# HGRN values in a decoder layer on one Trainium2 core: blocks read back from memory and transposed on VectorE, in place of TensorE transposes

## The chip, the core and the metric

The kernel runs on one core of one Trainium2 chip. The metric is the device time of one execution in microseconds (us). All arithmetic is in 32-bit floats; TensorE products are made of two-part splits of their operands (a rounded part and the rest), three matmuls for each block.

Short names: PE is TensorE (matmul, and the transpose as a matmul with an identity), PEld its weight load, DVE is VectorE, ACT is ScalarE, POOL is GpSimd, SP is SyncE, which issues the DMAs here.

## What is computed

One inference step of a decoder layer, for a prompt of T = 1024 tokens and for 8 single-token samples (NT = 1032 columns together, ND = 8):

```
proj = rmsnorm(x) @ w_in                      # 1024 -> q, f, i, g, z, xbc, dt
f = lb + (1-lb)*sigmoid(f);  k = 1-f;  q = silu(q);  v = i
# HGRN2, 8 heads of 128 x 128: gated linear recurrence
S_t = f_t * S_{t-1} + k_t v_t^T;    o_t = S_t^T q_t
o = rmsnorm(o) * silu(g)
# Mamba-2 SSD, 16 heads, conv + scan -> y
x = x + concat(o, y) @ w_out
x = x + (silu(conv(gate)) * val) @ w_down     # ConvFFN
```

The outputs are y, the new HGRN and SSM states, and the conv states. The change concerns v of the HGRN heads.

## The kernel before

**Layout.** Activations lie feature-major: partitions are features, columns are the 1032 tokens. The input projection is cut into jobs of 128 output features. A job has three chunks of 344 columns, and for each chunk 24 matmuls `mm<-hh,wh`, `mm<-hl,wh`, `mm<-hh,wl` (line 93). `head_in(h)` (L800) makes four jobs for HGRN head h: f, q, v and sg. Each evicts its chunks by an ACT activation (L812); the f job ends with `f_end`, which makes k.

**A head.** `head(h, t)` (L823) is a generator that works through one head in stages. It starts with the 8 decode columns of v: a transpose on PE into the bank vd (L828), a DVE copy (L836), a DMA to memory `vd_d<-vd` (L837), and later two loads `vb<-vd_d` that spread the rows over all partitions for the sample states. Then the 1024 prompt columns of v: eight PE transposes of 128x128 (L833), four to a PSUM bank `vtp`, and two ACT copies of 128x512 (L834) into `vt[0]` and `vt[1]`: token-major blocks, partitions are the 128 tokens of a block and columns its 128 features.

The head then multiplies q by f (L895, DVE, into v's buffer, as v is no more needed), and builds the masked score blocks `am` level by level: products and scalings on DVE (L866, L867, L872), small matmuls `a` on PE, masks on DVE (L891, L902). After them come the transposes of k, and `vt` is used for the first time as the right-hand side of the state matmuls `kv` (L952), later as the left-hand side of the output matmuls `o` (L977). The head ends with its own RMS norm: POOL multiplies twice (L996), and SP writes the result, `mix_d<-sg` (L1001).

**What sets the order.** PE's order is written out by hand: `drive` (L266, called at L1113) advances the head's generator and, at each `yield w`, lets a share of the projection's matmuls go between. Next to head h stand the jobs of head h+1. Next to head 7 stand the first jobs of the output projection, o8.0 to o12.2 (`out_job`). The other engines' orders are set by the scheduler, each engine's instructions run in that order, and so do the DMA issues on SP.

**Output projection.** `o8.0` is the first job that reads `mix_d`, the concatenated mixers' outputs, blocks 8 to 11 of 128 features (the SSM part). `mix_load` fetches four blocks k0 to k3 in three column chunks each: twelve loads `ml<-mix_d` of 172 KB (L175), each split by an ACT cast `mh<-ml` (L1011) and a DVE subtraction `ml<-ml,mh` (L1012). The buffers are those of `hh` and `hl`, which become free as the last projection job (sg of head 7) ends with them. `fetch` is a DMA on SP that is placed after the latest weight load; a weight load is `ws` (L189, 512 KB), with an ACT cast `wh<-ws` (L190) and a DVE subtraction `wl<-ws,wh` (L192).

The functions that the diff touches, and what calls them:

Of the kernel before, what the change touches and what calls it, by code (L numbers as in the profile page):

```python
# [8 lines left out]
F32 = mybir.dt.float32  # L9
# [7 lines left out]
P = 128  # L17
DM = 1024
T = 1024
# [5 lines left out]
H = 8  # L25
SH = 16
CHUNK = 128
NC = T // CHUNK
# [22 lines left out]
def hybrid_layer(  # L51
# [9 lines left out]
    V, A, G, PE, SP = nc.vector, nc.scalar, nc.gpsimd, nc.tensor, nc.sync  # L61
# [5 lines left out]
    dram = ctx.enter_context(tc.tile_pool(name="dscr", bufs=1, space=DRAM))  # L67
# [3 lines left out]
    def nm(s):  # L71
        cnt[0] += 1
        return f"{s}_{cnt[0]}"
# [8 lines left out]
    def tl(tag, name, dt=F32):  # L82
        w, n = TAGS[tag]
        return (work if tag in ("hT", "big", "e", "g") else tmp).tile([P, w], dt, tag=tag, bufs=n, name=nm(name))

    def half(name):
        return tl("s", name)[:, :512]

    def bank(s, tag="mx"):
        return psmx.tile([P, 512], F32, tag=tag, bufs=NBANK[tag], name=nm(s))  # L90
# [65 lines left out]
    ident = keep.tile([P, P], F32, name="ident")  # L156
# [15 lines left out]
    def fetch(dst, src):  # L172

        with tc.issue_after(last_w[0].ins):
            SP.dma_start(dst, src)  # L175
# [50 lines left out]
    def job(name, load, run):  # L226
        jobs.append((name, load, run))
# [51 lines left out]
    def w_in(off):  # L279
        return lambda: wload(w_in_[0, :, off:off + P], KT)  # L280

    def steps(w, m0, m1, hi, lo, cs, out):
        kt = len(hi)
        for k in range(kt):
            for i, (a, x) in enumerate(((w[0], hi), (w[0], lo), (w[1], hi))):
                mm(out, a[:, k, m0:m1], x[k][:, cs], start=(k == 0 and i == 0), stop=(k == kt - 1 and i == 2))
                if k < kt - 1 or i < 2:
                    yield True

    def in_job(name, off, evict, begin=None, end=None):  # L290
        def run(w):
            if begin is not None:
                begin()
            for c, cs in enumerate(chunks):
                ps = psmm.tile([P, 512], F32, tag="mm", name=nm("mm"))[:, :CH]
                yield from steps(w, 0, P, hT_hi, hT_lo, cs, ps)
                evict(c, cs, ps)
                if c == NCH - 1 and end is not None:
                    end()
                yield True  # L300
        job(name, w_in(off), run)

    def in_job_last(name, off, evict, begin):

        def run(w):
            begin()
            ps = [psmm.tile([P, 512], F32, tag="mm", name=nm("mm"))[:, :CH] for _ in chunks]
            for k in range(KT):
                for c, cs in enumerate(chunks):
                    for i, (a, x) in enumerate(((w[0], hT_hi), (w[0], hT_lo), (w[1], hT_hi))):  # L310
                        mm(ps[c], a[:, k, :], x[k][:, cs], start=(k == 0 and i == 0), stop=(k == KT - 1 and i == 2))
                        if k < KT - 1 or i < 2:
                            yield True
                    if k == KT - 1:
                        evict(c, cs, ps[c])
                        yield True
        job(name, w_in(off), run)
# [109 lines left out]
    for c, cs in enumerate(chunks):  # L427
        ps = psmm.tile([P, 512], F32, tag="mm", name=nm("dt"))
# [9 lines left out]
    for i in range(9):  # L438
        n = P if i < 8 else ND
# [85 lines left out]
    for g in range(4):  # L525
        rows = slice(32 * g, 32 * g + 32)
# [203 lines left out]
    def once(work):  # L730
        def run():
# [19 lines left out]
    G.affine_select(eye8, eye8, pattern=[[1, ND], [-1, ND]], compare_op=ALU.is_equal, fill=0.0, base=0,  # L751
                    channel_multiplier=0)
    vd_d = dram.tile([H, ND, P], F32, name="vd_d")

    am = const.tile([P, NC, P], F32, name="am")
    G.memset(am, 0.0)
# [10 lines left out]
    blk = [slice(i * P, (i + 1) * P) for i in range(4)]  # L767
# [32 lines left out]
    def head_in(h):  # L800
        t = {}

        def f_end():
            f, k = t["f"], tl("big", "k")
            A.activation(f[:, :NT], f[:, :NT], AF.Identity, bias=lbt[:, 0, h:h + 1], scale=lbt[:, 1, h:h + 1])
            V.tensor_scalar(k[:, :NT], f[:, :NT], -1.0, 1.0, op0=ALU.mult, op1=ALU.add)
            t["k"] = k

        for n, off, func in (("f", OFF_F, AF.Sigmoid), ("q", OFF_Q, AF.Silu), ("v", OFF_I, AF.Copy),
                             ("sg", OFF_G, AF.Silu)):  # L810
            def evict(c, cs, ps, n=n, func=func):
                A.activation(t[n][:, cs], ps, func)  # L812

            def begin(n=n):
                t[n] = tl("e" if h == 0 and n == "f" else "big", n)

            if h == H - 1 and n == "sg":
                in_job_last(f"{n}{h}", off + h * P, evict, begin)
            else:
                in_job(f"{n}{h}", off + h * P, evict, begin, f_end if n == "f" else None)  # L820
        return t

    def head(h, t):  # L823
        f, k, q, v, sg = (t[n] for n in ("f", "k", "q", "v", "sg"))
# [3 lines left out]
        PE.transpose(dps[:ND, :P], v[:, T:NT], ident)  # L828
        vt = [half("vt"), half("vt")]
        for hf in range(2):  # L830
            ps = bank("vtp")
            for i in range(4):
                PE.transpose(ps[:, blk[i]], v[:, hf * 512 + i * P:hf * 512 + (i + 1) * P], ident)  # L833
            A.copy(vt[hf], ps)  # L834
        vd = small.tile([ND, P], F32, tag="vd", name=nm("vd"))
        V.tensor_copy(vd, dps[:ND, :P])  # L836
        SP.dma_start(vd_d[h], vd)  # L837
# [75 lines left out]
        ps = bank("a3")  # L913
# [9 lines left out]
        ps, p6 = bank("a5"), bank("a6")  # L923
# [11 lines left out]
            mm(ops[32 * g:32 * g + 32, :P], qb[:, b, :], Sds[b // 4][:, b % 4, :], start=(b < 4), stop=(b >= 4))  # L935
        odr = small.tile([P, P], F32, tag="odr", bufs=1, name=nm("odr"))
        V.tensor_copy(odr, ops[:, :P])
        yield 3.5

        for hf in range(2):  # L940
            kt[hf] = half("kt")
            ps = bank("ktp")
# [5 lines left out]
        for hf in range(2):  # L948
            SS[hf] = half("SS")
            ps = bank("kv")  # L950
# [20 lines left out]
        for hf in range(2):  # L971
            oh = sg[:, hb[hf]]
            ps = bank("o")
            for i in range(4):
                n = hf * 4 + i
                Sb, c = before[n], slice(n * P, (n + 1) * P)
# [14 lines left out]
        for hf, (oh, hl) in enumerate(hls):  # L991
            ps = bank("hms")
# [97 lines left out]
    heads = [None] * H  # L1090
    ssm_gate(0)
    heads[0] = head_in(0)
    ssm_gate(1)
    heads[1] = head_in(1)
    job("conv", None, once(lambda: spread(conv_states(), 60)))
    for h in range(2, H):
        heads[h] = head_in(h)
# [9 lines left out]
    with tc.manual_schedule(engines={mybir.EngineType.PE}):  # L1107
        finish("x3")
        drive(ssd(0), 45.5, "x7")
        drive(ssd(1), 45.5, "v0")  # L1110
        finish("z7")
        for h in range(H):
            drive(head(h, heads[h]), 32.0 if h else 35.0, f"sg{h + 1}" if h < H - 1 else "o12.2")  # L1113
        finish("o12.6")
        for r0 in (0, 4):
            mixes[r0] = mix_load(r0)
# [238 lines left out]
    with tc.manual_schedule(engines={mybir.EngineType.PE}):  # L1355
# [43 lines left out]
        def down(w, kt, msl, acts, c):  # L1399
            q = quarters[c]  # L1400
            ps = psmm.tile([P, 512], F32, tag="mm", name=nm("dn"))[:, :q.stop - q.start]
            for k in range(kt):
                hi, lo = acts[k]
                wh, wl = w(k)
                mm(ps, wh[:, msl], hi[:, q], start=(k == 0), stop=False)
                mm(ps, wh[:, msl], lo[:, q], start=False, stop=False)
                mm(ps, wl[:, msl], hi[:, q], start=False, stop=(k == kt - 1))
                tick()
            return ps

        acts = [act_load(k) for k in range(RND)]
        for r0 in range(0, FT - RND, RND):
            nk = min(RND, FT - r0)
            rows = slice(r0 * P, (r0 + nk) * P)
            nxt = [act_load(r0 + RND + k) for k in range(min(RND, FT - r0 - RND))]
            for m in range(0, KT, 2):
                wh, wl = wload(w_down[0, rows, m * P:(m + 2) * P], nk, 2 * P)
                for i in range(2):
# [3 lines left out]
                    for c, cs in enumerate(quarters):  # L1422
                        ps = down(lambda k: (wh[:, k, :], wl[:, k, :]), nk, slice(i * P, (i + 1) * P), acts, c)
# [14 lines left out]
    for c in (3, 0, 1, 2):  # L1438
        cs = quarters[c]
        for m in range(KT):  # L1440
            ps = down(lambda k: wd[k], nk, slice(m * P, (m + 1) * P), acts, c)
            V.tensor_tensor(xT[m][:, cs], xT[m][:, cs], ps, op=ALU.add)
        for t0 in range(cs.start, cs.stop, P):
            n = min(P, cs.stop - t0)
# [49 lines left out]
```

## Time and profile before

| what | value |
|---|---|
| time, median of 3 runs | 1772.98 us (1771.92 to 1773.81) |
| profiled execution, span | 1770.0 us |
| mean granted clock of the core | 0.996 |
| v's transposes on PE (L833) | 64 instructions, 8.3 us busy |
| v's ACT copies (L834) | 16 instructions, 8.5 us busy |
| DMA packets | 220325, 190.76 MB, mean 108 GB/s |

The profile is one execution taken by the hardware profiler. "Busy" is time in which an engine works, instructions that overlap counted once. In a timeline row stand the start, the length of the group, the engine, the line, the operation with out<-in, the shape and the count; a bracket at the end gives the idle time of that engine just before the row, and what ended it. SPq rows are the issues of DMAs by SP's queue, not the transfers. In a windows row stand the stretch, its length, busy time and count for PE, PEld, DVE, ACT and POOL, the granted clock of PE (1.00 is full speed), the busy share of the core's 16 DMA engines, and GB/s.

### The profile page before, as it was taken

The page shows a single profiled execution, that of the slowest core. Times are in us where ns is not written, and L with a number is a line of the kernel's source. Part 1 is how long each engine was busy: PE and PEld are TensorE (multiplying, and loading weights), DVE is VectorE, ACT ScalarE, POOL GpSimd, SP SyncE. Part 2 cuts the span into 40 slices and gives each one's busy share as a digit, 9 for nine tenths or more (in the row PEclk, how much of TensorE's full clock was granted, in tenths as well). Part 3 has the DMA queues.
Part 4 walks back from the last instruction along what each step waited for, and adds up shares of the span by engine and source line. Part 5 has one row for each costly group of instructions (what it writes and reads, how often), then busy time and mean ns, then how long its engine had stood idle before and what let it go on. Part 6 is the DMA issues. An engine that isn't in the chain of part 4 may idle for free. (4 is left out here: it accounts for less than half of the span.)

```text
span 1770.0 us, 38596 instructions
## 1 busy us (share of the span) xinstructions
PE 1720.0 (97%) x16143; PEld 1672.4 (94%) x16143; DVE 1121.0 (63%) x2021; ACT 822.8 (46%) x1472; POOL 476.3 (27%) x477
## 2 busy tenths in 40 slices
PE   7999899999999999999999999999999999999997
PEld 6998798999999999999899989999999999999997
DVE  6667966565554564567746688776666767444545
ACT  7677688454544555455423374343333434111114
POOL 2103331120110110111100355666666664000002
PEclk9999999999999999999999999999999999999999
DMA  4144635542222221234336742222222225422212
GB/s 155 40 127 126 183 99 149 177 136 96 75 83 58 85 75 51 77 97 139 115 108 204 243 128 73 72 84 83 86 73 73 82 82 213 152 85 78 92 61 97
DMA packets 220325, 190.76 MB, mean 108 GB/s; under 512 B 13644, under 2 KB 195414, under 8 KB 220134
## 3 DMA queue, kind: packets, MB, share of 16 engines
q1 hardware_dynamic: 219862, 188.19, 34.0%
q8 instruction: 127, 2.08, 0.5%
q14 instruction: 48, 0.39, 0.1%
q0 software_dynamic: 288, 0.10, 0.0%
HBM read 145.72 MB, written 42.71 MB: 106 GB/s over the span
## 5 line engine op out<-in xcount | busy, mean ns | idle before, releaser
L93 PE MATMUL mm<-hh,wh 128*128 128x344 f32 x1248 | 406.9, 327 | 0.6 <-ACT sz L672 0.6
L93 PE MATMUL mm<-hl,wh 128*128 128x344 f32 x1248 | 406.0, 326 | 0.0
L93 PE MATMUL mm<-hh,wl 128*128 128x344 f32 x1248 | 403.7, 324 | 0.0
L93 PEld LDWEIGHTS mm<-hh,wh 128*128 128x128 f32 x1248 | 236.4, 190 | 4.2 <-issue 2.0
L93 PEld LDWEIGHTS mm<-hl,wh 128*128 128x128 f32 x1248 | 236.6, 190 | 2.4 <-issue 0.9
L93 PEld LDWEIGHTS mm<-hh,wl 128*128 128x128 f32 x1248 | 236.5, 190 | 2.0 <-issue 1.2
L190 ACT CAST wh<-ws 128x1024 fp32r<-128x1024 f32 x96 | 100.5, 1047 | 237.4 <-PE dn L93 135.5
L93 PE MATMUL ub<-uh,wh 128*128 128x258 f32 x704 | 199.3, 283 | 3.1 <-DVE fext L1307 2.7
L93 PE MATMUL ub<-ul,wh 128*128 128x258 f32 x704 | 199.0, 283 | 0.0
L93 PE MATMUL ub<-uh,wl 128*128 128x258 f32 x704 | 198.7, 282 | 0.0
L93 PE MATMUL dn<-ah,wh 128*128 128x256 f32 (+1 forms) x640 | 181.2, 283 | 2.1 <-DVE x L1424 2.1
L93 PE MATMUL dn<-al,wh 128*128 128x256 f32 (+1 forms) x640 | 180.6, 282 | 0.0
L93 PE MATMUL dn<-ah,wl 128*128 128x256 f32 (+1 forms) x640 | 180.1, 281 | 0.0
L192 DVE TENSOR_TENSOR wl<-ws,wh 128x1024 fp32r<-128x1024 f32 x88 | 115.6, 1313 | 72.1 <-ACT wh L190 71.1
L93 PE MATMUL ua<-uh,wh 128*128 128x258 f32 x528 | 149.6, 283 | 1.9 <-DVE val L1319 1.2
L93 PE MATMUL mm<-mh,wh 128*128 128x258 f32 x512 | 146.5, 286 | 3.5 <-DVE x L1054 2.1
L93 PE MATMUL ua<-ul,wh 128*128 128x258 f32 x528 | 149.3, 283 | 0.0
L93 PE MATMUL ua<-uh,wl 128*128 128x258 f32 x528 | 148.3, 281 | 0.0
L93 PE MATMUL mm<-mh,wl 128*128 128x258 f32 x512 | 145.0, 283 | 0.9 <-issue 0.9
L93 PE MATMUL mm<-ml,wh 128*128 128x258 f32 x512 | 145.1, 283 | 0.7 <-DVE ml L1012 0.7
L93 PEld LDWEIGHTS ub<-uh,wh 128*128 128x128 f32 x704 | 132.9, 189 | 3.7 <-DVE fext L1307 2.9
L1257 DVE TENSOR_TENSOR wl<-wt,wh 128x512 fp32r<-128x512 f32 x88 | 90.1, 1043 | 70.0 <-ACT wh L1256 69.7
(355 smaller groups left out, 4070.0 us busy)
## 6 DMA issues: line engine op xcount, KB each, us to landing
ws<-in_w_in_dram SPq DMA_DIRECT2D x52, 512.0 KB
ws<-in_w_up_dram SPq DMA_DIRECT2D x44, 512.0 KB
ws<-in_w_out_dram SPq DMA_DIRECT2D x24, 512.0 KB
act_d<-val SPq DMA_DIRECT2D x22, 516.0 KB
al<-act_d SPq DMA_DIRECT2D x22, 516.0 KB
ws<-in_w_down_dram SPq DMA_DIRECT2D x22, 512.0 KB
ml<-mix_d SPq DMA_DIRECT2D x48, 172.0 KB
csb<-cs_d SPq DMA_DIRECT2D x32, 256.0 KB
```

The lines of the kernel that those rows point to most:

```text
L93: PE.matmul(out, lhsT, rhs, start=start, stop=stop)
L190: A.copy(wh[:, :n], ws[:, :n])
L192: V.tensor_tensor(wl[:, :n], ws[:, :n], wh[:, :n].bitcast(F32), op=ALU.subtract)
L1257: V.tensor_tensor(lo[:, cs], sums[name], hi[:, cs].bitcast(F32), op=ALU.subtract)
```

## The change

When the last chunk of v has been evicted, the new `v_end` writes the prompt columns of v to memory in four DMAs, one for each group of 32 partitions (features). The order in memory is [32 j, 8 chunks c, 4 token groups a, 128]: j is the feature's place in its group of 32, and the 128 are the four feature groups with 32 tokens each. So each DMA writes 1024 pieces of 32 tokens of one feature (128 B), which swaps 32x32 blocks as wholes and leaves each block as it is. At the start of a head, eight loads fetch [32 j, 4 chunks, 128] (rows of 512 B) into a group of 32 partitions of `vt`; after them, VectorE transposes each 32x32 block of `vt[0]` and `vt[1]` in place, which leaves the token-major blocks as before. The PE transposes of the prompt columns, their two PSUM banks and the two ACT copies for each head are gone. The 8 decode columns go as before.

```diff
+    vb_d = dram.tile([H, 32, NC, 4, P], F32, name="vb_d")
...
+        def v_end():
+            for b in range(4):
+                SP.dma_start(vb_d[h, :, :, :, 32 * b:32 * b + 32].rearrange("j c a r -> j (c a) r"),
+                             t["v"][32 * b:32 * b + 32, :T].rearrange("j (n r) -> j n r", r=32))
+
+        ends = {"f": f_end, "v": v_end}
...
-                in_job(f"{n}{h}", off + h * P, evict, begin, f_end if n == "f" else None)
+                in_job(f"{n}{h}", off + h * P, evict, begin, ends.get(n))
...
         vt = [half("vt"), half("vt")]
         for hf in range(2):
-            ps = bank("vtp")
-            for i in range(4):
-                PE.transpose(ps[:, blk[i]], v[:, hf * 512 + i * P:hf * 512 + (i + 1) * P], ident)
-            A.copy(vt[hf], ps)
+            for a in range(4):
+                rows = slice(32 * a, 32 * a + 32)
+                fetch(vt[hf][rows].rearrange("j (c n) -> j c n", n=P), vb_d[h, :, 4 * hf:4 * hf + 4, a, :])
...
         V.tensor_copy(odr, ops[:, :P])
+        for hf in range(2):
+            V.transpose(vt[hf], vt[hf])
         yield 3.5
```

## The prediction

> **What bounds the kernel now.** I read the page's head first (busy shares, the clock line), then the windows view over the stretch in which the HGRN heads run, then the timelines of PE, SP, ACT, DVE and POOL around the start of a middle head (head 3) and of the last one (head 7).
>
> ```profile
> span 1770.0 us, 38596 instructions
> PE 1720.0 (97%) x16143; PEld 1672.4 (94%) x16143; DVE 1121.0 (63%) x2021; ACT 822.8 (46%) x1472; POOL 476.3 (27%) x477
> PEclk9999999999999999999999999999999999999999
> 416.00:829.00 413.00, 412.04 (x5270) 399.70 (x5257) 229.53 (x425) 206.74 (x335) 53.05 (x38) 1.00 0.26 78
> 826.00:890.00 64.00, 59.93 (x877) 56.99 (x876) 50.34 (x103) 28.08 (x60) 8.89 (x7) 1.00 0.41 127
> ```
>
> The window rows give start:end, length, busy PE, PEld, DVE, ACT, POOL, the granted clock, the DMA share and GB/s. From 416 to 829 (from early in head 0 to the start of head 7) PE is busy for 412.04 of 413.00 us at clock 1.00: PE alone bounds the heads, and what leaves its queue leaves the time. From 826 to 890, in head 7, PE idles 64.00 - 59.93 = 4.07 us: there it already meets other limits. The three runs have a median of 1772.98; the profiled span is 1770.0, so about 3 us lie around the span, and I add 3 to what I work out for it.
>
> **What is removed: PE transposes and ACT copies.**
>
> ```profile
> L833 PE MATMUL vtp<-ident,v 128*128 128x128 f32 x64 | 8.3, 272 | 0.0
> 582.04 1.03 PE L833 MATMUL vtp<-ident,v 128*128 128x128 f32 x8
> 582.83 0.40 PE L93 MATMUL mm<-hh,wh 128*128 128x344 f32 x1
> 385.36 1.04 PE L833 MATMUL vtp<-ident,v 128*128 128x128 f32 x8
> 388.30 0.84 PE L93 MATMUL ms<-gacc,ones 128*128 128x344 f32 x2 [1.91 <-DVE vd L836]
> 825.45 1.04 PE L833 MATMUL vtp<-ident,v 128*128 128x128 f32 x8
> 826.25 0.37 PE L93 MATMUL mm<-mh,wh 128*128 128x258 f32 x1
> ```
>
> Each transpose lasts 272 ns, but they overlap: the eight of head 3 start at 582.04 and the next matmul at 582.83, so they hold PE 0.79 us (0.80 in head 7). In head 0 PE waits 1.91 us right behind them, for a DVE copy that waits for no transpose of v; the gain there is about nothing at that place, and I allow 0.5 us for the small waits that follow in that head. Heads 1 to 6: 6 x 0.79 = 4.7. Together **-5.2 us** for heads 0 to 6; head 7's 0.80 is inside the count below. The 16 ACT copies (L834) leave an engine that is busy 46% and bounds nothing here: I count them at nothing.
>
> **What is added on DVE.** Two in-place transposes of 128x512 for each head. The built order puts them among the first scalings and masks of the head, ahead of its later part.
>
> ```profile
> 585.29 1.21 DVE L895 TENSOR_TENSOR v<-q,f 128x1024 f32<-128x1024 f32 x1
> 586.42 0.68 DVE L872 TENSOR_TENSOR tt<-f 128x512 f32<-128x512 f32 x1
> 595.18 0.46 DVE L891 COPY_PREDICATED amc<-mlow,a 128x256 f32<-128x256 uint8 x1 [1.47 <-PE a L93]
> ```
>
> No row shows this instruction. Bounds by the nearest rows: 0.68 us (128x512 elements) and 1.21 (twice that), so 1.4 to 2.4 us for a head; I take 0.68 each, the row of the same size. DVE idles 1.47 us ahead of 595.18 in the same stretch, which covers 1.4; without that cover PE's next near matmuls wait, at most 2.4 - 1.5 = 0.9 us a head, 6 us in all. I take nothing and keep +6 for the range's upper end.
>
> **What is added in transfers.** For each head, four writes of v in 4096 pieces of 128 B, and eight loads of 64 KB in 1024 rows of 512 B, all issued by SP in its order.
>
> ```profile
> 442.00:446.00 4.00, 4.00 (x33) 4.00 (x32) 2.09 (x4) 2.93 (x5) 0.00 (x0) 1.00 0.46 131
> q1 hardware_dynamic: 219862, 188.19, 34.0%
> 566.67 0.44 ACT L812 ACTIVATE v<-mm 128x344 f32<-128x344 f32 x1
> 568.05 0.37 SPq L189 DMA_DIRECT2D ws<-in_w_in_dram  x1
> 581.43 2.86 POOL L996 TENSOR_TENSOR sg<-sg,sq 128x512 f32<-128x512 f32 x2 [49.21 <-DVE sq L653]
> 582.55 0.29 SPq L837 DMA_DIRECT2D vd_d<-vd  x1
> 584.31 0.34 SPq L1001 DMA_DIRECT2D mix_d<-sg  x1
> 585.39 0.38 SPq L189 DMA_DIRECT2D ws<-in_w_in_dram  x1
> 585.87 1.11 SPq L175 DMA_DIRECT2D vb<-vd_d  x2
> 581.97 1.05 ACT L190 CAST wh<-ws 128x1024 fp32r<-128x1024 f32 x1 [1.45 <-PE mm L93]
> ```
>
> In the window 442 to 446 little but one 512 KB weight load moves (131 GB/s x 4 us = 524 KB, 1024 pieces of 512 B): 0.46 x 16 x 4 / 1024 = 29 ns a piece. The mean over the queue is 0.34 x 16 x 1770 / 219862 = 43.8 ns. No row shows 128-B writes. At 29 ns the writes of a head take 4096 x 29 / 16 = 7.4 us of the engines, at 43.8 they take 11.2, at twice the mean 22.4. I take 7.4, by the row nearest in size. Loads: 1024 x 29 / 16 = 1.9 us.
>
> The cover in heads 1 to 6: v's last eviction ends at 566.67 + 0.44 = 567.11; in the built order the loads of vt stand on SP behind mix_d<-sg, which waits for POOL's end (584.29). That leaves 17.2 us, and 7.4 or 11.2 fit. The eight loads then hold SP for 8 issues at about 0.45 (the twelve ml loads below take 5.57 us): 584.7 to 588.2, and vt lands about 2.3 later, at 590.5. DVE's rows before 595.18 leave it idle from 593.7, so two transposes that wait until 590.5 still find time there. What is queued behind on SP: vd_d (582.55 becomes 588.2), then ws (585.39 becomes 588.7) and vb. A weight load has room: ws issued at 568.05 stands well before the cast at 581.97, which PE, not the DMA, released. The decode work behind vb is wanted only at the head's end. So heads 1 to 6 pay nothing.
>
> The Trainium skill, "DMA: Bandwidth & Descriptors", section "Specifications", says that transfers below 512 B make the DMA engine read, modify and write. Worked out as two passes of a 29 ns piece, an estimate, that is 58 ns and 14.8 us a head, 2.4 us inside the cover of 17.2 where my 7.4 has 9.8; by that rule alone the sum stays, but the rival of slow writes, below, would come near (I would give it 0.2). No trace here shows a write of 128 B.
>
> **What is moved: head 7's SP queue.** In before, SP issues all twelve ml<-mix_d (the four input blocks k0 to k3 of o8.0, three chunks each) before head 7 starts, from 814.51, and only then mix_d<-sg of head 6. In the built order of after it stands thus: out<-SS, four vb_d writes, ml k0 twice, **mix_d<-sg of head 6**, eight vt, vd_d, four ml (k1, k1, k0, k1), ws, three ml k2, ws, three ml k3. So ten of the twelve ml loads fall behind a wait for POOL. PE's order is written out: the first job of head 7 is o8.0, and its first group goes through k0 to k3.
>
> ```profile
> 814.51 5.57 SPq L175 DMA_DIRECT2D ml<-mix_d  x12
> 823.57 3.12 POOL L996 TENSOR_TENSOR sg<-sg,sq 128x512 f32<-128x512 f32 x2 [45.30 <-ACT mh L1011]
> 826.71 0.32 SPq L1001 DMA_DIRECT2D mix_d<-sg  x1
> 827.54 0.28 PE L93 MATMUL mm<-ml,wh 128*128 128x258 f32 x1
> 816.83 0.90 ACT L1011 CAST mh<-ml 128x344 fp32r<-128x344 f32 x2 [0.19 <-DMA ml<-mix_d]
> 817.35 0.52 DVE L1012 TENSOR_TENSOR ml<-ml,mh 128x344 fp32r<-128x344 f32 x1
> 832.76 0.38 SPq L189 DMA_DIRECT2D ws<-in_w_out_dram  x1
> 833.24 1.88 SPq L175 DMA_DIRECT2D ml<-mix_d  x4
> 837.12 1.42 ACT L1011 CAST mh<-ml 128x344 fp32r<-128x344 f32 x3 [0.60 <-DMA ml<-mix_d]
> 830.16 0.76 PE L93 MATMUL a<-v,k 128*32 128x32 f32 x64 [0.33 <-DVE v L895]
> 833.22 0.39 PE L93 MATMUL mm<-ml,wh 128*128 128x258 f32 x1 [0.67 <-DVE ml L1012]
> ```
>
> In before's clock: POOL ends at 826.7; with ten of the mh and ml splits gone from ACT and DVE ahead of it I take mix_d at 826.2. Eight vt, 826.6 to 830.2; vd_d at 830.2; four ml from 830.5; ws at 832.3; three ml k2 from 832.7; ws at 834.1; the first k3 at **834.5** (0.45 for each issue, as 5.57 / 12 gives).
>
> From issue to the cast an ml took 816.83 - 814.51 = 2.3 us with the engines free and 837.12 - 833.24 = 3.9 behind one ws. Here two ws and three ml stand before it. By the window 442 to 446 a ws holds the engines 0.46 x 4 = 1.84 us, and an ml of a third of that size 0.6: from the first ws's issue, 1.5 us until it flows (2.3 less an ml's time, roughly), then 1.84 + 1.8 + 1.84 + 0.6 give 839.9. The three prices put k3's landing at 836.8, 838.4 and 839.9; I take 839.0. Then cast and subtraction (about 0.5 each): PE's k3 can start at 840.0 where it stood at 827.54: 12.5 us later. PE waits for 0.33 and 0.67 us just behind that are swallowed: **+11.5 us**. With the first price it is 9.3, and if all 4.07 us of idle between 826 and 890 goes, 6.2; with the last, 12.4, and 13.5 with one more us of issue.
>
> **Sum:** 1770.0 - 5.2 + 11.5 = 1776.3, plus 3 around the span: **1779.0 us**, 0.3% slower. Its own range is 1774 (6.2) to 1787 (13.5, and half of DVE's +6).
>
> **Rivals.**
> - *The loss is taken up again (faster).* PE's lateness is paid only as far as what follows is bound by PE. The place is head 7 and the out jobs behind it: PE idles 4.07 us up to 890, and more if DMA and DVE work there goes on while PE stands. It decides once more than 11.5 - 5.2 = 6.3 us are regained. With everything regained the time is 1773 - 5.2 = 1767.5. For it: DVE is busy 50.34 of 64 us there and PE waits for it. Against: PE's gaps there sum to less than the loss, and the rest of the jobs are matmuls in a fixed order.
> - *The small writes are slow (much slower).* From 17.2 us a head on (4096 / 16 x 67 ns) vt's first load waits on SP for the writes, and with it vd_d and ws; from about 20 us DVE's transposes are late and hold the scalings that PE waits for. At 22.4 us that is some 5 us a head less 1.47 of idle, 7 x 3.5 = 25: 1800. For it: 128 B is a quarter of the smallest piece priced above. Against: it needs over twice the 29 ns.
> - *The change gains where I price a loss at half (no difference).* If k3 lands early (9.3) and 3 to 4 us are regained, the sum is -5.2 + 5.7: 1773.5.
>
> **Chances.** Forecast 0.66, regained 0.11, no difference 0.13, slow writes 0.10. A measurement of this kernel can tell about 0.2% (3.5 us) from no change. Faster by more: 0.11 + 0.02; within: 0.13 + 0.03 of the forecast's low end; slower: the rest. The range reaches down to the regained case, 1767, and up to 1787; above it lies most of the slow writes.
>
> **What would show it.** Right: in the changed trace head 3's transpose of the decode columns (vd) is followed directly by the next matmul; PE from 416 to head 7 is busy as before; SP shows ml k1 to k3 behind mix_d<-sg and vt, and PE a wait of some 12 us in o8.0's first group, ended by the split of ml. Wrong: waits of PE for DVE in every head (transposes late or long), casts of wh that a DMA ends, or no wait in o8.0.

## The result, and the profile after

The changed kernel takes 1784.39 us (median of 4 runs, 1782.27 to 1787.99) where the kernel before takes 1773.26 (4 runs, 1771.92 to 1773.81): ratio 1.0056, 95% interval 1.0038 to 1.0074. The profiled execution has a span of 1780.5 us where before's has 1770.0, so 10.5 us are to be found.

The head of the page of the changed kernel, and its windows for the stretch from early in head 0 to the start of head 7 and for the 16 us behind it (columns as in the prediction: start:end, length, busy PE, PEld, DVE, ACT, POOL, granted clock, DMA share, GB/s):

```profile
span 1780.5 us, 38672 instructions
PE 1716.0 (96%) x16079; PEld 1666.7 (94%) x16079; DVE 1137.9 (64%) x2037; ACT 815.6 (46%) x1456; POOL 487.1 (27%) x477
416.00:821.00 405.00, 402.27 (x5256) 390.13 (x5256) 244.45 (x430) 195.09 (x310) 62.74 (x38) 1.00 0.35 92
826.00:838.80 12.80, 2.77 (x7) 1.64 (x7) 6.15 (x16) 3.86 (x9) 0.00 (x0) 0.52 0.87 272
```

The heads' stretch is shorter (405 us to the start of head 7 where before has 409), and PE is busy for nearly all of it (2.2 of the 2.7 us of idle in that window are two waits in head 0, at 417.9 and 419.1, which before has too, at 414.6 and 415.8, just ahead of its window). From 826 to 838.8 PE works 2.77 us of 12.8. To see where the two executions part, take the start of one instruction in both, PE's transpose of the decode columns (`vd`), and subtract:

| place | before | after | difference |
|---|---|---|---|
| vd of head 0 | 385.25 | 385.79 | +0.54 |
| vd of head 1 | 455.30 | 456.99 | +1.68 |
| vd of head 3 | 581.93 | 581.71 | -0.22 |
| vd of head 5 | 703.23 | 701.37 | -1.86 |
| vd of head 7 | 825.34 | 821.12 | -4.22 |
| last norm matmul of head 7 (`hms`) | 880.54 | 890.10 | +9.56 |
| last product of the kernel (`dn`) | 1760.11 | 1770.48 | +10.37 |

Heads 1 to 6 give 5.90 us (from +1.68 to -4.22), head 7 takes 13.8 (from -4.22 to +9.56), and the rest (1.68 up to head 1, and 0.81 from `hms` to `dn`) adds 2.5 us. A difference of that size up to head 1 is also seen without any change: the run only_h7 below, whose heads 0 to 6 are before's, goes from +2.27 at vd of head 0 to -0.49 at vd of head 1. PE's timeline of the changed kernel at head 3 and at head 7:

```profile
581.71 0.27 PE L835 MATMUL vd<-ident,v 128*8 128x128 f32 x1
581.73 0.40 PE L93 MATMUL mm<-hh,wh 128*128 128x344 f32 x1
...
821.12 0.27 PE L835 MATMUL vd<-ident,v 128*8 128x128 f32 x1
823.14 0.38 PE L93 MATMUL mm<-mh,wh 128*128 128x258 f32 x1 [1.75 <-ACT mh L1019]
824.88 0.39 PE L93 MATMUL mm<-ml,wh 128*128 128x258 f32 x1 [1.35 <-DVE ml L1020]
830.14 0.58 PE L93 MATMUL mm<-mh,wh 128*128 128x258 f32 x1 [4.76 <-ACT mh L1019]
835.85 0.58 PE L93 MATMUL mm<-mh,wh 128*128 128x258 f32 x1 [4.36 <-ACT mh L1019]
838.74 0.58 PE L93 MATMUL mm<-mh,wh 128*128 128x258 f32 x1 [1.54 <-ACT mh L1019]
```

At head 3 the projection goes on directly behind vd. At head 7 the first group of o8.0 stops at each of the blocks k0 to k3: the four rows with `mh` are k0, k1, k2 and k3. The releaser named is ACT's cast; for k1 to k3 ACT itself waited for the loads, as its timeline shows (`mh<-ml`, ended by `DMA ml<-mix_d`). For k0 it did not: its cast at 822.61 follows a cast of wh without idle time. But k1 came only at 830.14, so that k0's waits add nothing.

```profile
829.61 0.94 ACT L1019 CAST mh<-ml 128x344 fp32r<-128x344 f32 x2 [6.14 <-DMA ml<-mix_d]
835.32 1.40 ACT L1019 CAST mh<-ml 128x344 fp32r<-128x344 f32 x3 [2.60 <-DMA ml<-mix_d]
838.21 1.44 ACT L1019 CAST mh<-ml 128x344 fp32r<-128x344 f32 x3 [1.49 <-DMA ml<-mix_d]
```

And SP's queue, with POOL's last row ahead of it, says why the loads were late:

```profile
806.73 3.91 SPq L812 DMA_DIRECT2D vb_d<-v  x4
810.74 1.19 SPq L175 DMA_DIRECT2D ml<-mix_d  x2
819.34 2.84 POOL L1004 TENSOR_TENSOR sg<-sg,sq 128x512 f32<-128x512 f32 x2 [37.40 <-issue]
822.20 0.32 SPq L1009 DMA_DIRECT2D mix_d<-sg  x1
822.71 4.04 SPq L175 DMA_DIRECT2D vt<-vb_d  x8
826.84 0.28 SPq L843 DMA_DIRECT2D vd_d<-vd  x1
827.23 1.76 SPq L175 DMA_DIRECT2D ml<-mix_d  x4
829.03 0.43 SPq L189 DMA_DIRECT2D ws<-in_w_out_dram  x1
829.56 1.40 SPq L175 DMA_DIRECT2D ml<-mix_d  x3
831.06 0.38 SPq L189 DMA_DIRECT2D ws<-in_w_out_dram  x1
831.54 3.70 SPq L175 DMA_DIRECT2D ml<-mix_d  x4
```

Two ml loads go out at 810.74; then SP stands still for over 10 us, with its head instruction mix_d<-sg waiting for POOL, which ends at 822.18, and ten loads that wait for nothing but free buffers stand behind it.

### The profile page after: what moved, and what is told of

Its sections match the earlier page's. It is cut to its first block, busy times and chain, and to the rows that moved or that the text cites. A ratio compares the mean times of both kernels' runs of the same rounds, so it can differ in the third digit from the quotient of the medians.

```text
span 1780.5 us, 38672 instructions
## 1 busy us (share of the span) xinstructions
PE 1716.0 (96%) x16079; PEld 1666.7 (94%) x16079; DVE 1137.9 (64%) x2037; ACT 815.6 (46%) x1456; POOL 487.1 (27%) x477
```

## The experiments

The theory: the new path itself gains what PE's transposes held, and the whole loss is the place of o8.0's input loads in SP's order at head 7. The rivals: the small writes and the loads cost time everywhere (traffic), VectorE's transposes do, or the lost clock does. In the edits `by_mem` is true for the heads that go by memory (write, loads and VectorE transposes); the others have the code of before. The kernel before was timed beside each group of runs: 1774.06 us beside h7_tensor, only_h7, h1_6 and ml_first, 1774.71 beside writes7, nowrite7, fill and h7_tensor_pe, 1774.9 beside the other four; ratios are to these.

### Head 7 back to TensorE (h7_tensor)

```diff
+        by_mem = h < H - 1
```

> Heads 0 to 6 go by memory and VectorE, head 7 as before. Theory (the whole loss is head 7's input blocks of o8.0 standing on SP behind mix_d<-sg and vt): SP issues all twelve ml ahead of mix_d<-sg again, PE has no wait of over 2 us at the start of head 7. In the changed kernel's trace the heads 1 to 6 had gained 5.9 us by the start of head 7 (from +1.7 to -4.2 against before), head 0 had lost 1.7; so about 1773.3 - 4.2 = 1769. Rival A (the small writes and loads, or VectorE's transposes, cost time everywhere and head 7 only shows it): no less than 1780.

Measured: 1770.84 us, ratio 0.9978 (0.9966 to 0.9989). The loss turns into a gain. SP's timeline of this kernel has the loads in one piece again, ahead of mix_d<-sg:

```profile
809.92 5.56 SPq L175 DMA_DIRECT2D ml<-mix_d  x12
822.13 0.32 SPq L1017 DMA_DIRECT2D mix_d<-sg  x1
```

Rival A falls. The gain is less than at head 7's start, though: vd of head 7 is 4.59 us earlier than in before, `hms` only 1.25. PE's timeline has this wait of 2.99 us, where before has one of 0.90 behind the same copy, and ACT's timeline has its cause:

```profile
850.68 0.39 PE L93 MATMUL mm<-mh,wh 128*128 128x258 f32 x1 [2.99 <-ACT x L1068]
...
847.53 1.45 ACT L1027 CAST mh<-ml 128x344 fp32r<-128x344 f32 x3 [4.06 <-DMA ml<-mix_d]
```

PE waits for `x<-mm`, the copy that empties its bank, and this stands on ACT behind the cast of the next set of inputs (for o12.0), which comes when its DMA comes. What arrives earlier at that place waits there.

### Head 7 alone (only_h7)

```diff
+        by_mem = h == H - 1
```

> Heads 0 to 6 as before, head 7 alone by memory and VectorE. Theory: all of head 7's loss and none of the gain: in the changed kernel PE came 13.8 us later through head 7 (from -4.2 to +9.6), so 1773.3 + 13.8 = 1787, and PE waits of about 12 us in o8.0's first group. Rival A (traffic of all heads): a seventh or eighth of the loss, 1775.

Measured: 1785.29 us, ratio 1.0058 (1.0040 to 1.0075); a loss as large as the changed kernel's with one head in eight changed (1787 was expected). In its trace head 7 takes 13.2 us more (from -1.19 at vd to +11.96 at hms). What heads 1 to 6 gain in the changed kernel can't be seen between these two times (1.0056 and 1.0058): the changed kernel is 2.4 us ahead at hms (+9.56), but 0.5 behind at the last product (+10.37 for +9.89). Why it loses its lead there is open; the intervals are wide enough to hold a difference of 4 us.

### Heads 1 to 6 (h1_6, run twice)

```diff
+        by_mem = 0 < h < H - 1
```

> Heads 1 to 6 by memory and VectorE, heads 0 and 7 as before. Theory: what head 0 lost in the changed kernel (PE's wait for the copy of vd 4.2 us where it was 1.9, then half a clock) was caused by head 0's vt loads on SP ahead of a load of Sh that VectorE waits for; without them 1.7 us less than with head 0 changed: 1773.3 - 5.9 = 1767.4. Rival: head 0's loss is chance or has another cause; then the same time as with head 0 changed, about 1769.

Measured: 1767.60 us, ratio 0.9959 (0.9944 to 0.9975).

> The kernel of run h1_6 once more (heads 1 to 6 by memory and VectorE), as the base of the two runs beside it: again about 6 us under the kernel before, ratio 0.9959.

Measured again: 1769.69 us, ratio 0.9970 (0.9957 to 0.9982). In both this version beats both kernels. Head 0 has a run of its own, the next.

### Head 0 alone (only_h0)

```diff
+        by_mem = h == 0
```

> Head 0 alone by memory and VectorE. Theory: the wait for the copy of vd grows from 1.6 to 1.9 us to above 4, as SP has three vt loads and two weight loads ahead of a load of Sh that VectorE waits for; no gain is there to set against it: 2 to 3 us slower than before, 1776. Rival: the difference between the kernels with and without a changed head 0 was chance: 1773 to 1774.

Measured: 1773.92 us, ratio 1.0000 (0.9987 to 1.0014). My theory on head 0, 2 to 3 us slower, finds no support; by the interval a loss of up to 2.5 us isn't excluded. The wait for the copy of vd is longer in the trace (3.5 us, where before has 1.9), but no time can be seen to be lost. What h1_6 has over h7_tensor isn't shown to be head 0's.

### The write without the read (writes7)

As h7_tensor; head 7 in addition issues its four writes of v, which nothing reads.

```diff
-        ends = {"f": f_end, "v": v_end if h < H - 1 else None}
+        ends = {"f": f_end, "v": v_end}
```

> Heads 0 to 6 by memory and VectorE; head 7 keeps its TensorE transposes, yet writes v to memory too (four DMAs that nothing reads). Theory (the loss is the SP order that the planner writes behind the four writes, not the loads of vt or the VectorE transposes): the built order again has two ml ahead of mix_d<-sg and ten behind it, with two ws between and no vt; the first k3 is issued 11 places behind mix_d, about 6 us after PE's vd, lands 6.4 later as in the changed kernel, so PE's k3 starts 13 us after vd where it was 2.2: 10.8 us, of which some 2.5 are regained later; 1770.8 + 8 = 1779. Rival (the loads of vt and the transposes in head 7 cost it): as without the writes, 1771.

Measured: 1776.33 us, ratio 1.0011 (0.9999 to 1.0023), that is 5.5 us above h7_tensor. SP's timeline:

```profile
805.95 3.98 SPq L812 DMA_DIRECT2D vb_d<-v  x4
810.02 1.20 SPq L175 DMA_DIRECT2D ml<-mix_d  x2
821.43 0.32 SPq L1017 DMA_DIRECT2D mix_d<-sg  x1
821.85 0.29 SPq L850 DMA_DIRECT2D vd_d<-vd  x1
822.19 0.37 SPq L175 DMA_DIRECT2D ml<-mix_d  x1
822.61 0.45 SPq L189 DMA_DIRECT2D ws<-in_w_out_dram  x1
823.16 1.58 SPq L175 DMA_DIRECT2D ml<-mix_d  x3
825.30 0.38 SPq L189 DMA_DIRECT2D ws<-in_w_out_dram  x1
825.78 3.67 SPq L175 DMA_DIRECT2D ml<-mix_d  x7
```

Four DMAs that no one waits for are enough to turn SP's order. They and two ml are out by 811.2, and the next 10 us SP only waits: it isn't their time on the chip that holds the ml, it is the order written at build time. The loss came out smaller than I expected (1779), as k3 started 11.2 us behind vd and not 13. Nor is it the whole loss: between h7_tensor and the changed kernel lie 13.5 us.

### The read without the write (nowrite7)

Head 7 reads head 6's block here, so its v is another head's.

```diff
-        ends = {"f": f_end, "v": v_end}
+        ends = {"f": f_end, "v": v_end if h < H - 1 else None}
-                fetch(..., vb_d[h, :, 4 * hf:4 * hf + 4, a, :])
+                fetch(..., vb_d[min(h, H - 2), :, 4 * hf:4 * hf + 4, a, :])
```

> All heads by memory and VectorE, but head 7 writes nothing and reads head 6's block in place of its own (so its v is another head's). Theory: the built order has nine ml (k0 to k2) and five vt ahead of mix_d<-sg, then three vt, vd_d and the k3 loads, without a ws; k3 is issued 2.3 us behind mix_d, lands 2.5 later, PE's k3 starts 6.5 us after vd where the changed kernel has 17.6: 11 us less, of which 2.5 were regained there anyhow; 1784.4 - 8.5 = 1776. Rival (the vt loads and transposes themselves cost head 7 its time): 1784.

Measured: 1772.56 us, ratio 0.9993 (0.9984 to 1.0002), against 1.0056 for the changed kernel: without head 7's writes some 11 us are back, with the eight loads and the two VectorE transposes still there. SP has nine ml ahead of mix_d<-sg now, and only k3 behind it; PE waits once, 5.62 us, for k3:

```profile
811.07 4.15 SPq L175 DMA_DIRECT2D ml<-mix_d  x9
815.26 2.33 SPq L175 DMA_DIRECT2D vt<-vb_d  x5
823.31 0.34 SPq L1009 DMA_DIRECT2D mix_d<-sg  x1
823.69 1.85 SPq L175 DMA_DIRECT2D vt<-vb_d  x3
825.64 0.28 SPq L843 DMA_DIRECT2D vd_d<-vd  x1
826.02 1.29 SPq L175 DMA_DIRECT2D ml<-mix_d  x3
...
828.88 0.58 PE L93 MATMUL mm<-mh,wh 128*128 128x258 f32 x1 [5.62 <-ACT mh L1019]
```

k3 starts 828.88 - 821.90 = 6.98 us behind vd (6.5 expected; the time expected was 1776). It waits for POOL by way of mix_d<-sg, a DMA it has nothing to do with.

### The ml loads placed earlier in the code (ml_first)

```diff
         for h in range(H):
+            if h == H - 1:
+                mixes[8] = mix_load(8)
             drive(head(h, heads[h]), ...)
```

> All heads changed; the code of the ml loads of o8.0 stands ahead of head 7's start, so that the built SP order has mix_d<-sg, then ten ml with two vt and no ws among them, then the other vt. Theory: the first k3 is issued ten places behind mix_d, 822.2 + 10 x 0.45 = 826.7, lands 2.7 later, is split by 830.4, where PE's k3 started at 838.7: 8 us less, 1776. Rival (ACT or VectorE, not the issue order, holds the split): 1782 or more.

Measured: 1782.37 us, ratio 1.0039 (1.0024 to 1.0053). k3 starts 834.89 - 825.11 = 9.8 us behind vd where the changed kernel has 17.6, so the wait shrank by 7.8 as expected; the time did not follow, as 1776 was expected and by the time alone the rival (1782 or more) would stand. The trace speaks against the rival: the splits came earlier with the loads. Head 7 as a whole shrank from 13.8 to 8.7 only (from -0.24 to +8.45): behind its wait the changed kernel makes up 2.5 us (+12.12 at the first of the transposes of the residual, `xtp<-ident,xs`, and +9.57 at the last), this one nothing (+7.96, +8.46). The ratio is lower by 0.0017, and the two intervals overlap. The order sets the wait; how much of it ends in the time depends on what comes next.

### The clock kept up (fill)

```diff
         PE.transpose(dps[:ND, :P], v[:, T:NT], ident)
+        if h == H - 1:
+            ps = bank("warm")
+            for i in range(156):
+                PE.transpose(ps[:, blk[i % 4]], ident, ident)
```

> The changed kernel with 156 TensorE transposes of the identity (into a bank that nothing reads) behind head 7's vd, about 15.5 us in which PE waited before. Theory: the waits stay, k3 starts at the same time; but the granted clock, which was 0.50 to 0.57 from 826 to 842 and 0.81 to 846 in the changed kernel, stays at 1.00, so that the matmuls behind the wait run at full speed: about 2 us less, 1782.4. Rival (the clock row matters nothing since PE waits at that time): 1784.4 or, if the filling is too long, more.

Measured: 1781.67 us, ratio 1.0042 (1.0030 to 1.0055); the changed kernel's is 1.0056 (1.0038 to 1.0074), so the times don't tell them apart. The window 822 to 842 of the changed kernel, and the same window of this one:

```profile
822.00:842.00 20.00, 6.85 (x22) 5.00 (x22) 12.45 (x25) 8.05 (x18) 0.18 (x1) 0.61 0.84 271
```

```profile
822.00:842.00 20.00, 19.83 (x243) 19.40 (x243) 12.48 (x26) 7.81 (x18) 0.00 (x0) 1.00 0.81 262
```

The clock did stay up, and it does count. The changed kernel goes from k3's first matmul, at 838.74, to the first projection matmul behind the next two sets of score matmuls in 5.16 us; this one does in 3.44:

```profile
843.90 0.39 PE L93 MATMUL mm<-ml,wh 128*128 128x258 f32 x1
```

```profile
839.19 0.39 PE L93 MATMUL mm<-mh,wh 128*128 128x258 f32 x1
842.63 0.39 PE L93 MATMUL mm<-ml,wh 128*128 128x258 f32 x1
```

The matmuls are the same, and so the lower clock costs 1.7 us. Two things hide it. The filling ends only 17.05 us behind vd, so that k0 to k2 wait for it and k3 starts 18.28 behind vd where the changed kernel has 17.62; and at 845.42 PE ends a wait of 1.45 us that the changed kernel hasn't. By the last `hms` the two stand at +9.46 and +9.56. So this run doesn't measure in the time what the clock costs.

### The TensorE transposes kept beside the new path (h7_tensor_pe)

As h7_tensor, with the eight PE transposes of v of heads 0 to 6 still done, into banks that nothing reads, without the ACT copies.

```diff
             if by_mem:
+                ps = bank("vtp")
+                for i in range(4):
+                    PE.transpose(ps[:, blk[i]], v[:, hf * 512 + i * P:hf * 512 + (i + 1) * P], ident)
```

> Heads 0 to 6 by memory and VectorE, head 7 as before; in addition heads 0 to 6 keep the eight TensorE transposes of v (into banks that nothing reads), without the ACT copies. Theory: heads 1 to 6 are bound by PE alone, so each of them gives back what the transposes held, 0.79 us: 1770.8 + 4.7 = 1775.5. Rival (the gain of the heads came from the ACT copies or from the order of VectorE): 1771.

Measured: 1776.77 us, ratio 1.0008 (0.9999 to 1.0018), 5.9 us above h7_tensor. In its trace heads 1 to 5 keep step with before (vd of heads 1 and 6: +1.57 and +1.44). So the gain of these heads (1 to 5) is the time that PE's transposes held; the ACT copies, gone here too, bring nothing there. At head 6 this kernel gains 0.7 us all the same, which has another cause.

### VectorE's transposes three times (dve3)

As h1_6.

```diff
-                V.transpose(vt[hf], vt[hf])
+                for _ in range(3):
+                    V.transpose(vt[hf], vt[hf])
```

> As h1_6, with each of the VectorE transposes done three times in place (which ends in the same blocks): four more of 0.70 us in each of six heads. Theory (VectorE has about 1.2 us to spare at that stage, the idle row ahead of the next mask, and is otherwise the chain that PE's next small matmuls wait for): 2.8 us more work less 1.2 of idle, 1.6 us a head, some 9 us slower than h1_6. Rival (VectorE is off the path, as its 64% busy says): the same time.

Measured: 1768.68 us, ratio 0.9968 (0.9954 to 0.9983), the same as h1_6 beside it (0.9970). The theory that VectorE had only its 1.2 us of idle to spare falls. VectorE's timeline shows that the idle ahead of the mask is used up and no gap is left:

```profile
590.61 1.45 DVE L954 STREAM_TRANSPOSE vt<-vt 128x512 f32<-128x512 f32 x2
591.99 0.41 DVE L904 COPY_PREDICATED amc<-mlow,a 128x256 f32<-128x256 uint8 x1
```

But PE has no wait for it in these heads: its hand-written order puts enough projection matmuls ahead of the next score matmuls.

### The writes twice (writes2)

As h1_6, each write of v done again to a second place that nothing reads.

```diff
-            for b in range(4):
-                SP.dma_start(vb_d[...], ...)
+            for d in (vb_d, vb2_d):
+                for b in range(4):
+                    SP.dma_start(d[...], ...)
```

> As h1_6, with the four writes of v done twice, the second time to a place that nothing reads: 4096 more pieces of 128 B in each of six heads. Theory (the writes are far from any bound, 13 ns a piece, 3.3 us of the 16 engines a head, and 3 us of SP in a stretch with nothing due): the same time within 1.5 us. Rival (traffic of small pieces costs the weight loads time): 3 us or more slower.

Measured: 1774.34 us, ratio 1.0008 (0.9995 to 1.0021), 4.7 us above h1_6 beside it. The expectation failed, and at first sight the rival is right. In the windows view, a stretch with the eight writes of head 3's v and no weight load:

```profile
566.50:576.10 9.60, 9.60 (x68) 9.18 (x68) 4.49 (x10) 6.02 (x10) 0.00 (x0) 1.00 0.74 111
```

8192 pieces in 0.74 x 16 x 9.6 us are 13.9 ns a piece, and PE is busy throughout. The loss stands elsewhere: PE's longest wait in the heads is at the start of head 2, for VectorE's `v<-q,f`, and VectorE's timeline shows that this stands behind the whole norm of head 1, which itself waits behind the copy of vd:

```profile
523.75 0.76 PE L93 MATMUL a<-v,k 128*32 128x32 f32 x64 [3.22 <-DVE v L910]
...
515.86 0.28 DVE L851 COPY vd<-vd 8x128 f32<-8x128 f32 x1 [9.16 <-PE vd L837]
517.81 1.28 DVE L651 SCALAR_TENSOR_TENSOR nt<-hms,sq 128x512 f32<-128x512 f32 x2
521.41 2.28 DVE L910 TENSOR_TENSOR v<-q,f 128x1024 f32<-128x1024 f32 x1
```

In h1_6 that norm is done ahead of the copy of vd, without such an idle row. As in head 7: more writes, another order. From vd of head 2 to vd of head 3 this kernel goes from -3.00 to -0.60 against before, h1_6 from -2.34 to -3.22: 3.3 us are lost there. Heads 3 to 6 lose another 1.6 (this kernel goes on to -2.09 at head 7, h1_6 to -6.28), with waits of PE for the same `v<-q,f` of 0.3 us in three of them. What of this reaches the time is open.

## Why the prediction was right

1779.0 was forecast, 1784.39 measured: on the right side and inside the range, with the predicted place and mechanism, and the loss nearly twice as large (0.56% for 0.3%). Being inside the range owes something to a slip: 1770.0 - 5.2 + 13.5 + 3, with half of 6 us for DVE, gives 1784.3 as its upper end, not 1787, and the measured time lies 0.1 above that. (In the same way the middle sum is 1779.3.) The 3 us put around the span are 1.8 in the changed kernel's profiled run.

The sum had +6.3 us between the spans, the traces have 10.5. Of the 4.2 us between them head 7 has 2.3, the stretch up to head 1 has 2.2, what lies behind head 7 has 0.9, and heads 1 to 6 gave 1.2 back.

*Heads 0 to 6.* Forecast -5.2 at the start of head 7, measured -4.22: heads 1 to 6 gave 5.90 (4.7 forecast), in steps of 0.8 to 1.0 and one of 1.48; the 0.5 put down for head 0 wasn't there. The traces part by +1.68 up to head 1's vd; only_h7's trace, with the same code as before up to there, parts from before's by 2.76 between vd of head 0 and of head 1, so this can be chance, and only_h0 shows no cost (0.9987 to 1.0014). That the gain is PE's held time was shown by h7_tensor_pe, and the cost of nothing for ACT, DVE and transfers in these heads by h7_tensor, dve3 and the changed kernel's own steps.

*VectorE.* The transposes take 0.70 us each (0.68 taken). My +6 us for a longer one was no real danger: three times as many cost nothing (dve3).

*Writes.* I took 29 ns a piece; it is 13.9. The rival of slow writes needed 67. My estimate of 58 ns from the Trainium skill's rule for pieces below 512 B ("DMA: Bandwidth & Descriptors", section "Specifications") isn't borne out: a written piece of 128 B takes half of a loaded piece of 512 B here, not twice. For a byte it still takes about twice as long, which agrees with the 512 B that the same section of the Trainium skill gives as the least size for full rate.

*Head 7.* This is the term that was mis-sized: +11.5 forecast, +13.8 measured. In before's clock I had k3's issue 9.2 us behind vd (834.5 - 825.34) and its start on PE at 14.7; in the changed kernel the issue is at 831.54, 10.4 behind vd, and the start 17.6. So the issue was 1.3 later (mix_d<-sg 0.2, and the 19 issues from it to k3 took 9.3 us where I had 8.3), and from issue to start went 7.2 us, not 5.5. The prices of the pieces were not at fault, the count was: from the first ws to k3's cast (829 to 838.2 us) the DMA engines were busy for a share of 0.97 and moved 304 GB/s x 9.2 us = 2.80 MB, which is two ws and ten ml; the highest of the three prices had two ws and four ml. Three of the six others had been issued ahead of that ws, and three behind k3's first load. Two more terms were left out and partly cancel, which is luck: behind k3 the lower clock cost 1.7 us (fill), and 2.5 us were made up by the end of head 7. The order was read from the build, and held. That the writes bring this order about, and that the order costs time without head 7's loads and VectorE transposes (5.5 us of 13.5), was first shown by writes7 and nowrite7; the prediction had put down the order without its cause. k3 starts 2.1 us behind vd in h7_tensor, 11.2 with the writes alone, 7.0 with the loads alone, and 17.6 with both.

*The clock.* The prediction took it as 1.00 throughout. It fell to 0.5 in the wait, and the traces of fill and the changed kernel put its cost at 1.7 us: a term that the sum left out.

*The rival of regained time* lost: 2.5 of 16 us were regained by the end of head 7, and in h7_tensor what lies there took back 3.3 us of the heads' gain.

What stays open: why the planner puts the ml behind mix_d<-sg once four writes of small pieces stand ahead of them. The orders show that it does; no trace shows its own prices. A version with the new path in all heads and all twelve ml ahead of mix_d<-sg wasn't run.

## What to carry to other kernels

Where a scheduler writes the queues, read the order of the build around each place where a long-waiting instruction can land ahead of loads: a DMA that waits for an engine blocks everything behind it on its queue, and ten loads behind one store cost more here than all that the change gained. An added transfer that is cheap on the chip can still move others, so try it in the stages where nothing urgent shares its queue (here heads 1 to 6: 0.3 to 0.4% faster) before it goes into all.

## What the runs showed of the hardware that I had not expected

Contiguous pieces of 128 B, written from 32 partitions to memory, took 13.9 ns of a DMA engine each (writes2), half of the 29 ns of a 512-B piece of a weight load. In the changed kernel the granted clock was 1.00 up to 826.5, 5 us behind the last of the dense matmuls (821), then 0.50 up to 843.5, and 1.00 from there, 4.8 us after steady work began at 838.7. A VectorE transpose of 128x512 in 32x32 blocks took 0.70 to 0.72 us in the changed kernel, near the 0.68 or 0.69 of the quickest products of two 128x512 tensors there.
